# A hybrid decoder block with a PEER mixer: G tables requested half a group earlier, the residual fetched before the end, hidden products spread, 22 gathered rows moved to an earlier loop, and three places instead of four for the first 56 gathered rows

## The chip, the cores and the metric

The kernel runs on one core of a Trainium2 chip. The core has a matrix engine (TensorE, PE in the rows; its weight loads are PEld), a vector engine (VectorE, DVE), a scalar engine (ScalarE, ACT), GpSimd (POOL) and SyncE (SP), each with a queue of its own that it works off in order. Loads and stores between device memory and on-chip memory are issued on SP's and POOL's queues, and a few on ACT's. The metric is the device time of one execution in microseconds (us).

## The reference

The block works on 512 tokens of 1024 features (four tiles of 128 tokens). After the two token mixers comes the PEER channel mixer, which most of the change touches: each token picks 8 x 16 experts of 16384 by a product key, and

```
def block(args):
    xb, ib, gb = args
    hid = jnp.einsum('thkd,td->thk', u[ib], xb)
    a = jax.nn.gelu(hid.astype(jnp.float32), approximate=False) * gb
    return jnp.einsum('thk,thkd->td', a.astype(x.dtype), v[ib])
...
x = x + merged @ w_out[layer]
h2 = rms_norm(x, norm2_g[layer])
x = x + peer_ffn(h2, peer_wq[layer], peer_subkeys[layer], peer_u[layer], peer_v[layer])
```

Here `u` and `v` are tables of 16384 rows of 1024 float32 values, `ib` the indices of the picked experts and `gb` their gates.

## The kernel before

The kernel does PEER in two ways at once. For some products it gathers the picked rows, one row of `u` or `v` per token, 128 tokens at a time (512 KB a gather, an indirect DMA on POOL's queue, `row`), and multiplies on VectorE; for the others it streams all of `u` and `v` through TensorE, and a table G that holds the gates in a dense form picks what counts. Token tiles 0 and 3 have their `u` side by gathered rows, tile 3 its `v` side too; tiles 1 and 2 have both sides dense, tile 0 its `v` side.

Time falls into four parts.

1. The front of token tile 0 alone (norm, projections, HGRN2, attention, gates).
2. The front of tiles 1 to 3 (`Front`, `mixers`, `post`), weights streamed through `slot`. Beside it run the 128 gathered `u` rows of tile 0: after each weight load `background` lets the pump `rows` go on by 2.8 rows, up to 128. A gathered row needs a place on chip, given in turn from `row_places`: three buffers named rq and one named row. VectorE's product (`u_steps`, scalar_tensor_tensor with its sum into `hid`) frees the place. After the front, the three rq places take the PEER queries.
3. The hidden loop (`for b in range(NPRE)`, 72 steps): each step multiplies one block of 128 experts of `u` (`hidden`: tile ub, product ph, result pre). Beside it run the routing of the other tiles, the steps that build G (`scatter_steps`: tiles e, eg, pg, Gx; the table goes to device memory as g_d), and `ROWS_H` = 0.6 gathered `u` rows of tile 3 a step.
4. The down loop (`for b in range(NKEY)`, 128 steps): step b takes the slice b of G, which is loaded eight steps at a time (1.5 MB, tile Gc from g_d) into one of two buffers in turn, multiplies it by pre[b] in place (VectorE), splits it into two parts (ah on ScalarE, al on VectorE), loads a block of `v` (tile vb), splits it too (vh on ScalarE, vl on VectorE), and multiplies on TensorE: 18 matmuls of 512 columns into six accumulators acc. The remaining 56 hidden products (24 matmuls of 256 columns each, with ub split into uh and ul) run in the same loop, one a step in program order, and so do `ROWS_D` = 1.9 gathered rows a step, first the rest of the `u` rows, then the 128 `v` rows (`v_steps`).

After the loop three token tiles are finished in turn: the residual is read back from `out`, both accumulators of the tile are added on VectorE, and the tile is stored.

The order of the instructions on each engine is set when the program is built: a scheduler with a time model of its own takes the instructions in program order, moves one ahead where its model says that its inputs and its buffer are ready, and writes one fixed list for each engine. So a list can differ from the code's order, and at run time each engine waits at its next entry, whatever is ready behind it.

Of the kernel before, what the change touches and what calls it, by code (L numbers as in the profile page):

```python
# [8 lines left out]
F32 = mybir.dt.float32  # L9
# [9 lines left out]
P = 128  # L19
S = 512  # L20
D = 1024
# [6 lines left out]
NKEY = 128  # L28
# [13 lines left out]
VD = (1, 2, 0)  # L42
NU = len(UD) * P
GT = 16
NGT = len(VD) * P // GT
GB = 8
# [2 lines left out]

ROWS_F = 2.8  # L50

NPRE, RING = 72, 56

ROUTE1, ROUTE2, SCAT_H = 12, 30, 2
# [1 line left out]
GS = 4  # L56
ACTW = (4, 12)

ROWS_H, ROWS_D = 0.6, 1.9
UBUFS = 3  # L60
UK, WBUFS, WSBUFS, ATB = 4, 2, 4, 2

# [9 lines left out]
def kernel(ctx: ExitStack, tc: tile.TileContext, x, wst, par, cst, cols, g2, keys, u, v, ut, vr, out):  # L72
# [695 lines left out]
    rctx = ctx.enter_context(ExitStack())  # L768
    rt = rctx.enter_context(tc.tile_pool(name="rt", bufs=1, side="left", **TILE))
    pr = rctx.enter_context(tc.tile_pool(name="pr", bufs=1, space=PSUM, side="left"))  # L770
    row_places = [(rq_pool, "rq")] * 3 + [(gat, "row")]

    def background(load):
        rows(min(ROWS_F, P - rows.done))

    f = Front(tuple(range(1, 4)), True, background)
# [17 lines left out]
    def hidden(b, pool):  # L794
        if RING <= b < NPRE:

            if (b - RING) % 4 == 0:
                pre4[0] = rq_pool.tile([P, 4, NU], F32, name="rq") if b - RING < 12 else rq_pool.tile([P, 4, NU], F32, name="keys_sb", bufs=1)
            dst = pre4[0][:, (b - RING) % 4]
        else:  # L800
            dst = dp.tile([P, NU], F32, name="pre", bufs=RING)
        pre.append(dst)
        ub = us.tile([P, KC, P], F32, name="ub")
        nc.sync.dma_start(out=ub, in_=ut[b].rearrange("p (k i) -> p k i", k=KC))
        pt = pool.tile([P, NU], F32, name="ph")
        if b < NPRE:

            accumulate(pt, [ub[:, k] for k in range(KC)], h32, slice(None), True)
        else:
            ubs = halves(us.tile([P, KC, P], F32R, name="uh", bufs=1), us.tile([P, KC, P], F32R, name="ul", bufs=1), ub)  # L810
            accumulate(pt, [tuple(a[:, k] for a in ubs) for k in range(KC)], (hH, hL), slice(None), True)
        return nc.scalar.activation(dst, pt, AF.Gelu)  # L812

    with tc.tile_pool(name="hw", bufs=1, side="right", **TILE) as hw, \
            tc.tile_pool(name="gb", bufs=1, side="left", **TILE) as gb, \
            tc.tile_pool(name="php", bufs=3, space=PSUM, side="right") as php, \
            tc.tile_pool(name="pg", bufs=3, space=PSUM, side="right") as pg:
        pg_bank = lambda: pg.tile([P, 512], F32, name="pg")
        h32 = hw.tile([P, KC, NU], F32, name="h32")
        nc.vector.tensor_tensor(out=h32, in0=hH.bitcast(F32), in1=hL.bitcast(F32), op=ALU.add)  # L820
        scat.add(scatter_steps(0, pg_bank))
        routing(3, rq3)
        rows.add(u_steps(3))
        for b in range(NPRE):
            if b == ROUTE1:
                routing(1, rq1)
                scat.add(scatter_steps(1, pg_bank))
            if b == ROUTE2:
                routing(2, rq2)
                scat.add(scatter_steps(2, pg_bank))  # L830
            behind[:] = [hidden(b, php)]
            rows(ROWS_H)
            if b % SCAT_H == 0:
                scat(1)
        scat(P)
# [6 lines left out]
    ngu = NU // GT  # L842
    acc = [[pacc.tile([P, 512], F32, name=f"acc{t}{c}") for c in range(2)] for t in range(len(VD))]
    for b in range(NKEY):
        if b % GB == 0:
            Gc = Gcs[0]
            if b:
                Gc = (vs if b // GB % 2 else dp).tile([P, NGT, GB, GT], F32, name="Gc", bufs=1)
                nc.sync.dma_start(out=Gc, in_=g_d[:, :, b:b + GB])
        a = pre[b]  # L850
        gsl = Gc[:, :, b % GB]
        nc.vector.tensor_mul(gsl[:, :ngu], a.rearrange("p (g t) -> p g t", t=GT), gsl[:, :ngu])
        aH, aL = halves(vs.tile([P, NGT, GT], F32R, name="ah"), vs.tile([P, NGT, GT], F32R, name="al"), gsl)
        vb = vs.tile([P, D], F32, name="vb", bufs=3)
        nc.sync.dma_start(out=vb, in_=vr[b])
        vH = vs.tile([P, D], F32R, name="vh")
        behind[:] = [nc.scalar.activation(vH, vb, AF.Copy)]  # L857
        vL = vs.tile([P, D], F32R, name="vl")
        nc.vector.tensor_tensor(out=vL, in0=vb, in1=vH.bitcast(F32), op=ALU.subtract)  # L859
        for t in range(len(VD)):  # L860
            for i, (l, r) in enumerate([(aH, vH), (aH, vL), (aL, vH)]):
                for c in range(2):
                    nc.tensor.matmul(acc[t][c], l.rearrange("p g t -> p (g t)")[:, t * P:(t + 1) * P], r[:, c * 512:(c + 1) * 512],  # L863
                                     start=(b == 0 and i == 0), stop=(b == NKEY - 1 and i == 2))
        if b + NPRE < NKEY:
            hidden(b + NPRE, ph)
        rows(ROWS_D)
    rows(2 * S)
    for t, T in enumerate(VD):
        x1r = gat.tile([P, D], F32, name="row")  # L870
        nc.sync.dma_start(out=x1r, in_=out[T * P:(T + 1) * P])
        for c in range(2):
            cs = slice(c * 512, (c + 1) * 512)
            nc.vector.tensor_add(x1r[:, cs], acc[t][c], x1r[:, cs])
        nc.sync.dma_start(out=out[T * P:(T + 1) * P], in_=x1r)


def layout(inputs):
# [53 lines left out]
```

## Time and profile before

| | us |
|---|---|
| median of 3 runs | 1810.34 (1808.81 to 1812.05) |
| the profiled execution | 1805.38 |
| its span (first to last instruction) | 1803.5 |
| TensorE busy | 1639.0 (91% of the span) |
| VectorE busy | 1346.3 (75%) |
| ScalarE busy | 700.8 (39%) |

"Busy" is an average over parts with different limits. A busy TensorE is not one at its peak, since the ends of matmuls are modelled. In a row of idle time the name behind the arrow is what came last before the engine went on.

### The profile page before, as it was taken

What the parts mean: (1) busy time and instruction counts of PE and PEld (TensorE: products, weight loads), DVE (VectorE), ACT (ScalarE), POOL (GpSimd) and SP (SyncE); (2) the same over time, 40 slices, a digit from 0 to 9 for tenths busy, and PEclk for the clock granted to TensorE, in tenths of its full rate; (3) what the DMA queues carried; (4) which work ended last, traced back from release to release, by engine and by line L of the source; (5) the groups of instructions that cost most, each with busy time, mean ns of one, the idle gap of its engine ahead of it and who ended that gap; (6) DMA issues with size and microseconds to landing.
All of it is one profiled execution on the core that took longest, in us unless ns stands there. A gap on an engine that the chain in (4) does not pass through costs nothing.

```text
span 1803.5 us, 26810 instructions
## 1 busy us (share of the span) xinstructions
PE 1639.0 (91%) x9725; PEld 1450.2 (80%) x9725; DVE 1346.3 (75%) x2805; ACT 700.8 (39%) x1283; POOL 641.5 (36%) x502
## 2 busy tenths in 40 slices
PE   8998979789988799999899889999999999988995
PEld 7887968689877797888789877888888888867774
DVE  3113999989886669998985577787788887777774
ACT  3323434334344544523454553334344333323331
POOL 0000355766550004452442123334444444443330
PEclk9999979999989899999999999999999999989998
DMA  8776468788884336665667688999999998888885
GB/s 287 245 232 221 143 206 312 245 296 306 304 287 170 119 121 240 208 201 193 211 227 252 225 293 308 331 355 333 331 335 342 331 331 315 286 281 300 299 293 183
DMA packets 173380, 473.41 MB, mean 262 GB/s; under 512 B 14784, under 2 KB 62144, under 8 KB 173248
## 3 DMA queue, kind: packets, MB, share of 16 engines
q1 hardware_dynamic: 115840, 268.47, 43.9%
q0 software_dynamic: 55296, 201.35, 31.3%
q10 hardware_dynamic: 2112, 1.88, 0.3%
q8 instruction: 77, 1.26, 0.3%
q14 instruction: 55, 0.45, 0.1%
HBM read 442.80 MB, written 27.79 MB: 261 GB/s over the span
## 4 chain that ended last, share of the span: by engine, by line
PE 47%; DVE 25%; DMA 21%; issue 4%; ACT 2%; POOL 1%; DVEq 0%; POOLq 0%; ACTq 0%; SPq 0%
PE acc L863 18%; PE pp L110 16%; DMA Gc<-g_d 9%; PE ph L110 9%; DMA w<-in_wst_dram 2%; DMA rq<-in_u_dram,idx 2%; DVE e L687 2%; DVE rowx L648 2%; PE pg L701 2%; DMA rowx<-in_u_dram,idx 2%; DVE rq L648 1%; DVE row L648 1%; DVE eg L696 1%; DMA row<-in_u_dram,idx 1%; DVE wl L97 1%
## 5 line engine op out<-in xcount | busy, mean ns | idle before, releaser
L110 PE MATMUL ph<-h,ub 128*128 128x256 f32 x1152 | 265.4, 386 | 0.0
L863 PE MATMUL acc<-vl,ah 128*128 128x512 f32 x768 | 243.5, 398 | 18.0 <-DVE vl L859 18.0
L863 PE MATMUL acc<-vh,al 128*128 128x512 f32 x768 | 244.3, 396 | 0.0
L110 PEld LDWEIGHTS ph<-h,ub 128*128 128x128 f32 x1152 | 219.2, 195 | 29.8 <-issue 0.2
L863 PE MATMUL acc<-vh,ah 128*128 128x512 f32 x768 | 221.1, 396 | 9.8 <-ACT vh L857 9.8
L636 POOL DMA_INDIRECT rowx<-in_u_dram,idx x96 | 122.7, 1278 | 216.1 <-ACT pre L812 56.8
L636 POOL DMA_INDIRECT rowx<-in_v_dram,idx x96 | 130.7, 1362 | 193.2 <-DVE h2g L667 90.2
L863 PEld LDWEIGHTS acc<-vl,ah 128*128 128x128 f32 x768 | 145.2, 192 | 49.3 <-DVE vl L859 20.8
L863 PEld LDWEIGHTS acc<-vh,ah 128*128 128x128 f32 x768 | 143.9, 191 | 38.8 <-ACT vh L857 11.1
L863 PEld LDWEIGHTS acc<-vh,al 128*128 128x128 f32 x768 | 146.5, 192 | 30.5
L96 ACT ACTIVATE ah<-Gc 128x384 fp32r<-128x384 f32 x128 | 67.0, 524 | 264.0 <-PE acc L863 261.3
L859 DVE TENSOR_TENSOR vl<-vb,vh 128x1024 fp32r<-128x1024 f32 x128 | 156.1, 1219 | 11.6 <-ACT vh L857 11.2
L857 ACT ACTIVATE vh<-vb 128x1024 fp32r<-128x1024 f32 x128 | 135.6, 1060 | 45.3 <-DMA vb<-in_vr_dram 44.5
L636 POOL DMA_INDIRECT rq<-in_u_dram,idx x96 | 120.0, 1250 | 93.5 <-DVE rq L648 52.9
L648 DVE SCALAR_TENSOR_TENSOR rowx<-rowx,h2g 128x1024 f32<-128x1024 f32 x96 | 122.4, 1276 | 39.2 <-DMA rowx<-in_u_dram,idx 39.1
L648 DVE SCALAR_TENSOR_TENSOR rq<-rq,h2g 128x1024 f32<-128x1024 f32 x96 | 132.8, 1385 | 19.8 <-DMA rq<-in_u_dram,idx 19.6
L96 ACT ACTIVATE wh<-w 128x512 fp32r<-128x512 f32 x144 | 89.1, 629 | 128.8 <-PE pp L110 71.1
L110 PE MATMUL ph<-hH,ul 128*128 128x256 f32 x448 | 127.6, 285 | 5.1 <-DVE ul L97 5.1
L110 PE MATMUL ph<-hH,uh 128*128 128x256 f32 x448 | 127.8, 285 | 3.8 <-ACT pre L812 3.8
L667 DVE SCALAR_TENSOR_TENSOR h2g<-rowx,hid,h2g 128x1024 f32<-128x1024 f32 x95 | 121.7, 1281 | 8.4 <-DMA rowx<-in_v_dram,idx 8.0
L110 PE MATMUL ph<-hL,uh 128*128 128x256 f32 x448 | 127.7, 285 | 0.0
L701 PE MATMUL pg<-eg,e 128*128 128x128 f32 x768 | 104.5, 290 | 23.5 <-DVE eg L696 17.3
(289 smaller groups left out, 3611.9 us busy)
## 6 DMA issues: line engine op xcount, KB each, us to landing
ub<-in_ut_dram SPq DMA_DIRECT2D x128, 512.0 KB, 4.7
vb<-in_vr_dram SPq DMA_DIRECT2D x128, 512.0 KB, 7.1
w<-in_wst_dram SPq DMA_DIRECT2D x107, 512.0 KB, 5.2
g_d<-Gx SPq DMA_DIRECT2D x24, 960.0 KB, 4.6
Gc<-g_d SPq DMA_DIRECT2D x15, 1536.0 KB, 16.5
wh<-in_wst_dram SPq DMA_DIRECT2D x37, 256.0 KB, 4.9
wl<-in_wst_dram SPq DMA_DIRECT2D x33, 256.0 KB, 5.4
pairB<-in_x_dram SPq DMA_DIRECT2D x5, 512.0 KB
```

What stands on the lines that cost most here:

```text
L96: nc.scalar.activation(hi, x, AF.Copy)
L97: (eng or nc.vector).tensor_tensor(out=lo, in0=x, in1=hi.bitcast(F32), op=ALU.subtract)
L110: nc.tensor.matmul(out, l, r, start=(k == 0 and i == 0), stop=(k == last and i == len(ops) - 1))
L636: d = nc.gpsimd.indirect_dma_start(out=r, out_offset=None, in_=src, in_offset=bass.IndirectOffsetOnAxis(ap=index, axis=0))
L648: nc.vector.scalar_tensor_tensor(r, r, 1.0, h2g[T], op0=ALU.mult, op1=ALU.mult, accum_out=hid[:, g, j:j + 1])
L667: nc.vector.scalar_tensor_tensor(acc, r, hid[:, g, j:j + 1], acc, op0=ALU.mult, op1=ALU.add)
L687: nc.vector.tensor_tensor(out=e1, in0=iota[:, None, :, 0].to_broadcast(by_token), in1=pk[:, ti, 0, tk, None].to_broadcast(by_token), op=AL ...
L696: nc.vector.tensor_tensor(out=eg, in0=e2.rearrange("p k q -> p q k"), in1=pkw[:, ti, tk, None].to_broadcast(by_token), op=ALU.mult)
L701: nc.tensor.matmul(pt[:, q], e1[:, q0 + q], eg[:, q0 + q], start=True, stop=True)
L857: behind[:] = [nc.scalar.activation(vH, vb, AF.Copy)]
L859: nc.vector.tensor_tensor(out=vL, in0=vb, in1=vH.bitcast(F32), op=ALU.subtract)
L863: nc.tensor.matmul(acc[t][c], l.rearrange("p g t -> p (g t)")[:, t * P:(t + 1) * P], r[:, c * 512:(c + 1) * 512], start=(b == 0 and i == 0 ...
```

## The change

Five things change. The load of a group of G is written at the middle of the group before it, not at the group's first step. The 56 hidden products of the down loop are spread so that the last is written at step 120 and not at step 55. From step 40 the hidden loop pumps 1.3 rows a step (`ROWS_L`) and no longer 0.6, which moves 22 rows out of the down loop, where 1.6 a step are pumped and no longer 1.9. The residual of the three last tiles is read back at step 123 into the buffers that gathered rows used, and each half of a tile is stored by itself. And the first 56 gathered rows beside the front of tiles 1 to 3 are given the three rq places in turn; the row place joins after them.

```diff
+RFEW = 56
-ROWS_H, ROWS_D = 0.6, 1.9
+ROWS_H, HLATE, ROWS_L, ROWS_D = 0.6, 40, 1.3, 1.6
+ULAST, XLAST = 120, 123
...
-    row_places = [(rq_pool, "rq")] * 3 + [(gat, "row")]
+    row_places = [(rq_pool, "rq")] * 3
     def background(load):
+        if rows.done >= RFEW and len(row_places) < 4:
+            row_places.append((gat, "row"))
         rows(min(ROWS_F, P - rows.done))
...
-            rows(ROWS_H)
+            rows(ROWS_H if b < HLATE else ROWS_L)
...
     for b in range(NKEY):
-        if b % GB == 0:
-            Gc = Gcs[0]
-            if b:
-                Gc = (vs if b // GB % 2 else dp).tile([P, NGT, GB, GT], F32, name="Gc", bufs=1)
-                nc.sync.dma_start(out=Gc, in_=g_d[:, :, b:b + GB])
+        if b % GB == GB // 2 and b + GB < NKEY:
+            g = b // GB + 1
+            Gcs.append((vs if g % 2 else dp).tile([P, NGT, GB, GT], F32, name="Gc", bufs=1))
+            nc.sync.dma_start(out=Gcs[g], in_=g_d[:, :, g * GB:(g + 1) * GB])
+        Gc = Gcs[b // GB]
...
-        if b + NPRE < NKEY:
-            hidden(b + NPRE, ph)
+        if len(pre) < NKEY and (len(pre) - NPRE) * ULAST <= b * (NKEY - NPRE):
+            hidden(len(pre), ph)
         rows(ROWS_D)
-    rows(2 * S)
+        if b == XLAST:
+            rows(2 * S)
+            x1s = []
+            for T in VD:
+                x1s.append(rx.tile([P, D], F32, name="rowx"))
+                nc.sync.dma_start(out=x1s[-1], in_=out[T * P:(T + 1) * P])
     for t, T in enumerate(VD):
-        x1r = gat.tile([P, D], F32, name="row")
-        nc.sync.dma_start(out=x1r, in_=out[T * P:(T + 1) * P])
         for c in range(2):
             cs = slice(c * 512, (c + 1) * 512)
-            nc.vector.tensor_add(x1r[:, cs], acc[t][c], x1r[:, cs])
-        nc.sync.dma_start(out=out[T * P:(T + 1) * P], in_=x1r)
+            nc.vector.tensor_add(x1s[t][:, cs], acc[t][c], x1s[t][:, cs])
+            nc.sync.dma_start(out=out[T * P:(T + 1) * P, cs], in_=x1s[t][:, cs])
```

Three places in the built lists. The first is VectorE's list around the multiplications of steps 96 to 103 (`Gc<-pre,Gc`). The first row is the last reader of the buffer that their load reuses, the al of step 87; the load on SP waits for it in both programs. Before:

```order
L97 TENSOR_TENSOR al<-Gc,ah 128x384
L859 TENSOR_TENSOR vl<-vb,vh 128x1024
L667 SCALAR_TENSOR_TENSOR h2g<-rowx,hid,h2g 128x1024
L667 SCALAR_TENSOR_TENSOR h2g<-row,hid,h2g 128x1024
L667 SCALAR_TENSOR_TENSOR h2g<-rowx,hid,h2g 128x1024
L97 TENSOR_TENSOR al<-Gc,ah 128x384
L859 TENSOR_TENSOR vl<-vb,vh 128x1024
L852 TENSOR_TENSOR Gc<-pre,Gc 128x16x16 x8
```

The same place in the changed program, from the same reader on:

```order
L102 TENSOR_TENSOR al<-Gc,ah 128x384
L867 TENSOR_TENSOR vl<-vb,vh 128x1024
L102 TENSOR_TENSOR al<-Gc,ah 128x384
L867 TENSOR_TENSOR vl<-vb,vh 128x1024
L860 TENSOR_TENSOR Gc<-pre,Gc 128x16x16 x8
L102 TENSOR_TENSOR ul<-ub,uh 128x1024
L672 SCALAR_TENSOR_TENSOR h2g<-rowx,hid,h2g 128x1024
```

Between the reader and the multiplications stood six instructions and now stand three. The table counts the same for all groups from the third on: what stands between the last reader of the buffer and the first multiplication (r a gathered row's product, V a vl, A an al, U a ul, ? the closing of the u rows), and how many r, V, A, U the list has from this group's first multiplication to the next group's.

| group (first step) | between, before | between, now | r,V,A,U before | r,V,A,U now |
|---|---|---|---|---|
| 16 | UVrAVrrUA | rVrArVAV | 15,9,8,5 | 13,8,8,3 |
| 24 | VrAVrUrAV | VrUrAVrAV | 14,8,8,5 | 13,8,8,4 |
| 32 | VrrAUrVAV | VrArVUrAV | 15,8,8,5 | 13,8,8,4 |
| 40 | VrAVrUrAV | rVrAVrUAV | 14,8,8,5 | 13,8,8,3 |
| 48 | VrAVrUrAV | VrUrAV?rAV | 14,8,8,5 | 12,7,7,4 |
| 56 | VrrAU?VrAV | rVUrAV | 14,8,8,5 | 13,8,8,4 |
| 64 | VrrUrAVAV | rVrAVU | 15,8,8,5 | 14,9,9,3 |
| 72 | rVrUrAVrAV | VrAVrAV | 13,7,7,5 | 12,7,7,4 |
| 80 | rVrUrAV | VrrUAV | 15,8,8,5 | 13,8,8,4 |
| 88 | VrUrArV | VrrAVU | 15,8,8,4 | 12,8,8,3 |
| 96 | VrrrAV | VAV | 13,9,9,0 | 13,7,8,4 |
| 104 | rVrArVAV | rVUA | 12,8,8,0 | 13,9,8,4 |
| 112 | VrArVrAV | rVrUAV | 11,8,8,0 | 13,8,8,3 |
| 120 | VrArVrAV | VrAV | to the end: 14 steps, no U | to the end: 15 steps, 4 U |

The second place is the end of the gathered rows of tile 0 on POOL's list, from the last split of a weight half (wl) to the first copy of the hidden loop. Before:

```order
L97 TENSOR_TENSOR wl<-w,wh 128x512
L636 DMA rq<-in_u_dram,idx 128x1024 x2
L636 DMA row<-in_u_dram,idx 128x1024
L636 DMA rq<-in_u_dram,idx 128x1024 x3
L636 DMA row<-in_u_dram,idx 128x1024
```

And in the changed program, from the last use of the row place on:

```order
L641 DMA row<-in_u_dram,idx 128x1024
L641 DMA rq<-in_u_dram,idx 128x1024 x3
L102 TENSOR_TENSOR wl<-w,wh 128x512
L641 DMA rq<-in_u_dram,idx 128x1024 x28
L710 COPY Gc<-Gx 128x128 x2
```

The scheduler uses the row place for later rows early, from the ninth gather on, and so the row place is spent when 31 rows are left. All in all 110 of the 128 gathers now use the three rq places, where 96 did. The third place is the end of SP's list; first before, after the last vb load but one group:

```order
L855 DMA vb<-in_vr_dram 128x1024 x14
L670 DMA row<-out_dram 128x1024
L672 DMA out_dram<-row 128x1024
L871 DMA row<-out_dram 128x1024
L875 DMA out_dram<-row 128x1024
L871 DMA row<-out_dram 128x1024
L875 DMA out_dram<-row 128x1024
L871 DMA row<-out_dram 128x1024
L875 DMA out_dram<-row 128x1024
```

And now:

```order
L863 DMA vb<-in_vr_dram 128x1024 x4
L883 DMA rowx<-out_dram 128x1024
L863 DMA vb<-in_vr_dram 128x1024 x2
L883 DMA rowx<-out_dram 128x1024 x2
L675 DMA row<-out_dram 128x1024
L863 DMA vb<-in_vr_dram 128x1024 x2
L677 DMA out_dram<-row 128x1024
L863 DMA vb<-in_vr_dram 128x1024 x4
L888 DMA out_dram<-rowx 128x512 x6
```

The three reads of the residual have moved among the last vb loads, and only six half stores stand behind them.

## Rows read from the trace of the kernel before

**Rows 1.** The page's head: span and busy time of each engine.

```profile
span 1803.5 us, 26810 instructions
PE 1639.0 (91%) x9725; PEld 1450.2 (80%) x9725; DVE 1346.3 (75%) x2805; ACT 700.8 (39%) x1283; POOL 641.5 (36%) x502
```

**Rows 2.** Busy time by stretch of the down loop (two stretches). Columns: stretch, its length, busy time and count of PE, PEld, DVE, ACT, POOL, then the granted clock, the DMA engines' share, GB/s.

```profile
1110.00:1480.00 370.00, 364.85 (x2034) 318.28 (x2035) 302.46 (x412) 144.04 (x202) 155.02 (x111) 1.00 0.93 332
1480.00:1660.00 180.00, 162.12 (x795) 136.71 (x794) 135.50 (x155) 58.50 (x81) 75.73 (x52) 0.95 0.84 294
```

**Rows 3.** The list of waits from 1050 us on: engine, line, what ended the wait, then total us, times, longest.

```profile
DVE Gc L852 <- DMA Gc<-g_d: 86.9, 15, 8.9
PE acc L863 <- DVE vl L859: 18.0, 6, 8.2
```

**Rows 4.** Timeline of VectorE and SP around three G loads (those of steps 88, 96 and, first row, 16; the last row is that of step 120). Columns: start, us, engine, line, what, and in brackets the idle time before and what ended it.

```profile
1111.67 0.43 DVE L852 TENSOR_TENSOR Gc<-pre,Gc 128x256 f32<-128x256 f32 x1 [8.62 <-DMA Gc<-g_d]
...
1529.65 0.55 DVE L97 TENSOR_TENSOR al<-Gc,ah 128x384 fp32r<-128x384 f32 x1
1530.23 0.53 SPq L849 DMA_DIRECT2D Gc<-g_d  x1
1537.08 1.22 DVE L859 TENSOR_TENSOR vl<-vb,vh 128x1024 fp32r<-128x1024 f32 x1
1545.94 1.10 DVE L852 TENSOR_TENSOR Gc<-pre,Gc 128x256 f32<-128x256 f32 x3 [7.64 <-DMA Gc<-g_d]
...
1580.69 0.53 SPq L849 DMA_DIRECT2D Gc<-g_d  x1
1596.93 2.77 DVE L852 TENSOR_TENSOR Gc<-pre,Gc 128x256 f32<-128x256 f32 x8 [8.87 <-DMA Gc<-g_d]
1602.55 1.22 PE L863 MATMUL acc<-vl,ah 128*128 128x512 f32 x2 [8.20 <-DVE vl L859]
...
1721.36 1.43 DVE L852 TENSOR_TENSOR Gc<-pre,Gc 128x256 f32<-128x256 f32 x4 [6.63 <-DMA Gc<-g_d]
```

**Rows 5.** Groups of VectorE instructions from 1110 to 1727 us: shapes, count, busy us, mean ns of one, idle before.

```profile
L859 DVE TENSOR_TENSOR vl<-vb,vh 128x1024 fp32r<-128x1024 f32 x106 | 129.2, 1219 | 8.3 <-ACT vh L857 8.0
L667 DVE SCALAR_TENSOR_TENSOR h2g<-rowx,hid,h2g 128x1024 f32<-128x1024 f32 x82 | 105.0, 1281 | 8.4 <-DMA rowx<-in_v_dram,idx 8.0
L97 DVE TENSOR_TENSOR ul<-ub,uh 128x1024 fp32r<-128x1024 f32 x49 | 59.8, 1220 | 10.4 <-ACT uh L96 10.1
L97 DVE TENSOR_TENSOR al<-Gc,ah 128x384 fp32r<-128x384 f32 x106 | 58.6, 553 | 16.4 <-ACT ah L96 9.3 <-PE acc L863 6.8
```

**Rows 6.** DMA issues: what, queue, count, KB each, median us from issue to landing; the last row is from the view of the line that loads Gc, over its 15 loads.

```profile
Gc<-g_d SPq DMA_DIRECT2D x15, 1536.0 KB, 16.5
rq<-in_u_dram,idx POOLq DMA_INDIRECT x96, 6.3
...
  DMA to landing us min/median/max: 15.2/16.5/18.0
```

**Rows 7.** TensorE in the down loop: two successive starts of the six vh-by-ah matmuls of a step without a hidden product (timeline), and one hidden product's 22 last matmuls on the chain that ended last.

```profile
1772.68 1.52 PE L863 MATMUL acc<-vh,ah 128*128 128x512 f32 x6
1776.76 1.52 PE L863 MATMUL acc<-vh,ah 128*128 128x512 f32 x6
...
1120.44 2.59 PE ph L110 x22
```

**Rows 8.** The end of the program on the timeline: the last matmuls, the adds, SP's stores and loads.

```profile
1783.31 1.29 DVE L874 TENSOR_TENSOR row<-acc,row 128x512 f32<-128x512 f32 x2 [4.03 <-PE acc L863]
1784.47 0.61 PE L863 MATMUL acc<-vh,al 128*128 128x512 f32 x2
1784.63 0.34 SPq L875 DMA_DIRECT2D out_dram<-row  x1
1787.26 0.33 SPq L871 DMA_DIRECT2D row<-out_dram  x1
1790.94 1.29 DVE L874 TENSOR_TENSOR row<-acc,row 128x512 f32<-128x512 f32 x2 [6.34 <-DMA row<-out_dram]
1799.73 0.34 SPq L875 DMA_DIRECT2D out_dram<-row  x1
```

**Rows 9.** The gathered rows beside the front of tiles 1 to 3, on the timeline: the gather with which the last 31 begin, a gather, its product, the place's next gather, a product that VectorE waited for, and the last product.

```profile
470.99 0.94 POOL L636 DMA_INDIRECT rq<-in_u_dram,idx  x1 [1.21 <-DVE rq L648]
...
502.28 1.15 POOL L636 DMA_INDIRECT rq<-in_u_dram,idx  x1 [1.60 <-DVE rq L648]
509.74 1.23 DVE L648 SCALAR_TENSOR_TENSOR rq<-rq,h2g 128x1024 f32<-128x1024 f32 x1 [1.04 <-DMA rq<-in_u_dram,idx]
512.09 1.21 POOL L636 DMA_INDIRECT rq<-in_u_dram,idx  x1 [0.30 <-DVE at L417]
...
542.01 1.23 DVE L648 SCALAR_TENSOR_TENSOR rq<-rq,h2g 128x1024 f32<-128x1024 f32 x1 [2.80 <-DMA rq<-in_u_dram,idx]
...
548.10 1.22 DVE L648 SCALAR_TENSOR_TENSOR row<-row,h2g 128x1024 f32<-128x1024 f32 x1
```

**Rows 10.** Busy time by stretch in the front of tiles 1 to 3 (first four rows) and in the hidden loop; columns as in Rows 2.

```profile
190.00:300.00 110.00, 94.86 (x667) 90.29 (x665) 106.68 (x297) 43.94 (x75) 59.26 (x45) 0.91 0.64 219
300.00:400.00 100.00, 80.83 (x535) 73.46 (x535) 92.49 (x179) 35.17 (x79) 68.16 (x52) 0.92 0.81 271
400.00:500.00 100.00, 99.00 (x780) 87.22 (x778) 86.69 (x169) 40.69 (x90) 60.50 (x49) 0.98 0.89 307
500.00:562.00 62.00, 48.57 (x318) 42.09 (x317) 53.76 (x102) 25.25 (x41) 22.67 (x19) 0.83 0.72 244
880.00:920.00 40.00, 36.85 (x200) 32.82 (x200) 39.62 (x130) 20.48 (x40) 16.58 (x14) 0.96 0.56 195
960.00:1024.00 64.00, 64.00 (x379) 58.60 (x378) 33.45 (x62) 34.13 (x75) 13.42 (x14) 1.00 0.71 233
```

## The prediction

> **What bounds the kernel now.** I read the page's head first: TensorE is busy 91% of the span of 1803.5 us, VectorE 75% [rows 1]. That alone would say "TensorE is the bound", so I looked stage by stage. In the down loop TensorE needs 4.08 us for a step's 18 matmuls (two successive starts, 1776.76 − 1772.68) and 24 × 2.59/22 = 2.83 us for a hidden product [rows 7]. Eight steps with five hidden products need 46.8 us; the groups' multiplications followed each other every 50 us around step 96, where almost no hidden product is left (1545.94 to 1596.93 is 51.0) [rows 4]. Something else sets that pace.
>
> The list of waits names it: VectorE stood 86.9 us for the loads of G, at 15 loads of 15 [rows 3]. The timeline shows why [rows 4]. After the last al that reads a G buffer (1529.65), SP issues the load into that buffer (1530.23); it lands 16.5 us later at the median, 15.2 to 18.0 [rows 6]; the eight multiplications of the new group stand only a few instructions behind that al in VectorE's list, so VectorE reaches them early and stands (7.64 us before 1545.94). Everything behind them waits too, the al that releases the next buffer among it. This is a ring: release, load, multiply, a group of vector work, release. Its period is
>
> (VectorE's work from one group's first multiplication to the next group's) − (the part that stands between release and multiplication) + 16.5.
>
> With a gathered product 1.28, vl and ul 1.22, al 0.55 [rows 5] and eight multiplications 2.77 [rows 4], group 80 has 15 r, 8 V, 8 A, 5 U = 42.2; between release and multiplication for group 88 stand 3 r, 2 V, U, A = 8.05; so 42.2 − 8.05 + 16.5 = 50.7. Group 88 to 96: 41.0 − 6.8 + 16.5 = 50.7, where the trace has 51.0. Over the 13 periods from group 16 to 120 the formula, with the counts of the table in the section on the change, gives 607.6; the trace has 1721.36 − 1111.67 = 609.7 [rows 4]. I trust it.
>
> **Loads ahead.** The load is written half a group earlier, but the built lists do not follow: SP still waits for the same al, the buffer's last reader, since there are two buffers in both programs. Cost and gain nil by themselves; what counts is the order on VectorE.
>
> **Down loop, groups 16 to 120.** What stands between release and multiplication shrinks at most groups (group 96: VrrrAV, 6.8, becomes VAV, 3.0; group 104: 8.6 becomes 4.3), and that part was work done during the load. The rows are fewer (13 a group for 14), but ul's stay to the end (3 to 4 a group, where before there were five and then none). Group 96 to 104 now: 13 r, 7 V, 8 A, 4 U and 2.77 = 37.2, less 4.3, plus 16.5 = 49.5 (before 43.3). The same for all, now: 43.9, 45.2, 45.2, 43.9, 45.2, 48.2, 49.5, 45.2, 48.2, 49.5, 49.5, 49.4, 49.5, together 612.3. TensorE's need per period, 8 × 4.08 + 3.5 × 2.83 = 42.5, is below each. Before, the first eight periods were 46.4 to 50.2, and the last three 43.3, 40.2, 38.9: the early gain is given back late. Term: 612.3 − 607.6 = +4.7. The period ahead (group 8 to 16), by the same formula, −1.3.
>
> **Down loop, its end.** From the multiplications of the last group on, TensorE's own work decides. Before, 1721.36 to the last matmul at 1785.1 [rows 4, 8] is 63.7 = 14 steps × 4.08 + 6.6 for a restart. Now 15 steps and four hidden products are left: 15 × 4.08 + 4 × 2.83 + 6.6 = 79.1. Term +15.4. Nothing hides it. That is where the spread of u is paid: not in work, but in hidden products that stand behind the last load and not in front of it. Loop in all: +18.8.
>
> **Tail.** Before, behind the last matmul come three rounds of read, two adds and a store in turn (the second round's adds start at 1790.94, 7.6 after the first's at 1783.31, having waited 6.34 for the read), the last store issued at 1799.73, and 3.8 us to the span's end at 1803.5 [rows 1, 8]. Now the reads are done earlier; six adds of 0.645 (1.29/2) from 1783.3 end at 1787.2; plus 3.8 is 1791.0. Term −12.5. The reads move in among the last vb loads; three of 512 KB against a G load's 1536 KB in 16.5 cost no more than one more such load there (bounds 0 to 16), and no G load is left behind them: I take 0.
>
> **Front of tiles 1 to 3.** In the built list 110 gathers and not 96 use the three rq places, and the last 31 use nothing else. A place goes round in product 1.2, reissue 0.3 to 1.1, landing 6.3 [rows 6, 9], 8.2 to 9.0 with the waits in line; the example takes 512.09 − 502.28 = 9.8. With three places that is 2.74 to 3.0 us a row, and 3.3 by the example. Now the last 31 rows run at (548.10 − 470.99)/31 = 2.49 [rows 9]. So they take 8 to 16 us longer, 24 by the example. VectorE already waits for such a gather (2.80 us at 542.01) [rows 9], and splits of the last weights stand behind the last product in its list, with TensorE behind them: between 500 and 562 TensorE is busy 48.6 of 62 us [rows 10]. Against that, VectorE is 97% busy at 190 to 300 (106.7 of 110) [rows 10] and paced by itself, so three places cost little there, and part of the end's loss is slack. Bounds 0 and 24; I take +9, near the lower price of the cycle.
>
> **Hidden loop.** Twenty-two more products of 1.22 to 1.28 come after step 40. From 960 on VectorE is busy 33.5 of 64 us and TensorE all of it: there they are hidden. But six of them stand between two of the G-building steps near 900, where VectorE is busy 39.6 of 40 [rows 10]: 6 × 1.22 = 7.3 if TensorE has no work ahead, 0 if it has. Were the later cover gone, all 22 would cost 27. I take +5, bounds 0 and 12.
>
> **Sum.** 18.8 − 12.5 + 9 + 5 = +20.3 on the profiled execution of 1805.4, that is 1825.7. The median of the three runs is 5 us above that execution, so I say 1830.
>
> **The rivals.** All but the last two terms hang on the landing time of G: each us of it is some 13 to 14 us, one for each period.
>
> 1. *The G loads land sooner: faster.* Fewer gathered rows run beside them (13 of 512 KB a group for 14 to 15) and fewer ub in the first half. The sign turns where the landing falls by 20.3/13.5 = 1.5 us, at 15.0. At 13.5 the time is 1830 − 40 = 1790. At 12 periods touch TensorE's 42.5, and no more is to be had than some 60. For it: the DMA engines were 93% busy up to 1480 and 84% after [rows 2], and the two late loads that I can read landed in 15.7 and 16.2. Against it: these two were below the median by 0.8 at most, although VectorE stood 7.6 and 8.9 us for them and asked for no new rows meanwhile [rows 4]; and from step 89 on ub loads now run beside G where none did. Chance 0.23.
>
> The Trainium skill (DMA: Bandwidth & Descriptors, section on SWDGE, HWDGE and iDMA) says that an engine goes round in turn among its internal queues, those fed by GpSimd apart from those fed by SP. By that a G load would speed up as soon as GpSimd's gathers run dry; an even half of the 294 GB/s of the late stretch would be an estimated 1.57 MB/147 = 10.7 us, and the loop TensorE's, some 60 us shorter. The trace does not bear this out, with 15.7 and 16.2 us for the late loads; other loads stand on SP's own queue.
>
> 2. *Front and hidden loop cost nothing* (slack takes both): 1830 − 14 = 1816. For: the idle 13 us of TensorE between 500 and 562. Chance 0.08.
>
> 3. *The places cost their full price*, 24, and the late reads of the residual hold a vb load up by some us: 1830 + 15 + 3 = 1848. For: the example cycle of 9.8. Chance 0.14.
>
> **Numbers.** My forecast, 1812 to 1846, has 0.55. 1830 is its middle. To hold 8 in 10, the range goes to half of rival 1's side and to rival 3: 1798 to 1849. What a measurement can tell from no change is 0.2%, 1806.7 to 1814.0. Faster takes nearly all of rival 1 (0.23) and a little more where terms fall together (0.02): 0.25; same 0.10, the margins of rivals 1 and 2 and my lower end; slower the rest, 0.65.
>
> **What would show it.** In the changed profile: VectorE's wait for G grows from 86.9 to about 115 us, at every load; periods of 44 to 49.5 with the late ones longest; landing at 16 to 17; hidden products near the last steps and 79 us from the last group's multiplications to the last matmul; 6 us from the last matmul to the end, not 18; the last product of the gathered rows some 9 us later than 548; a longer stretch around 900. I am wrong if the wait for G shrinks, if the last landing times are below 15, or if VectorE's order leaves TensorE enough work queued to ride through the stalls.

## The result and the profile after

The changed kernel is slower: 1824.9 us median for 1810.2 us before, ratio 1.0103, 95% interval 1.0073 to 1.0134. The forecast was 1830 us, with a range of 1798 to 1849. The size came out nearly as forecast, but two of the terms behind it were far off and cancelled, which was luck; so most of this section and the next is on where the time really went. Every ratio here is worked out over all executions in the faster of the chip's two states, and not from the medians (here 14.7 us apart); two of the six executions of e9_rows_moved were in the slower one, its profile among them.

The head of the changed kernel's page answers to [rows 1]:

```profile
span 1823.2 us, 26818 instructions
PE 1648.7 (90%) x9725; PEld 1454.9 (80%) x9725; DVE 1346.7 (74%) x2805; ACT 702.3 (39%) x1284; POOL 646.6 (35%) x502
```

The engines do the same work; what grew is time in which they stand, and, by 9.7 us, TensorE's busy time for the same 9725 matmuls. To find the place, I took the same instructions from the timeline of both kernels: the first gathered row of tile 0, the first matmul of the hidden loop, the first multiplication of the down loop, the last matmul. Before (the last matmul is in [rows 8], at 1784.47 + 0.61):

```profile
215.33 1.30 POOL L636 DMA_INDIRECT rq<-in_u_dram,idx  x1 [1.19 <-DVE idx L603]
650.38 1.99 PE L110 MATMUL ph<-h,ub 128*128 128x256 f32 x8
1048.82 1.43 DVE L852 TENSOR_TENSOR Gc<-pre,Gc 128x256 f32<-128x256 f32 x4 [3.20 <-POOL Gc L705]
```

After, with the last product of the gathered rows (583.43) and the six adds of the tail (1816.08):

```profile
222.87 1.30 POOL L641 DMA_INDIRECT rq<-in_u_dram,idx  x1 [1.20 <-DVE idx L608]
491.44 1.55 POOL L641 DMA_INDIRECT rq<-in_u_dram,idx  x1 [0.30 <-issue]
583.43 1.22 DVE L653 SCALAR_TENSOR_TENSOR rq<-rq,h2g 128x1024 f32<-128x1024 f32 x1
678.39 1.78 PE L115 MATMUL ph<-h,ub 128*128 128x256 f32 x7
1080.40 1.77 DVE L860 TENSOR_TENSOR Gc<-pre,Gc 128x256 f32<-128x256 f32 x5 [3.54 <-POOL Gc L710]
1816.08 3.68 DVE L887 TENSOR_TENSOR rowx<-acc,rowx 128x512 f32<-128x512 f32 x6 [3.80 <-PE acc L871]
1817.46 0.61 PE L871 MATMUL acc<-vh,al 128*128 128x512 f32 x2
```

| stretch | before | after | difference | forecast |
|---|---|---|---|---|
| to the first gathered row | 215.3 | 222.9 | +7.5 | 0 |
| on to the first hidden matmul | 435.1 | 455.5 | +20.5 | +9 |
| hidden loop | 398.4 | 402.0 | +3.6 | +5 |
| down loop, first multiplication to last matmul | 736.3 | 737.7 | +1.4 | +18.8 |
| last matmul to the end | 18.4 | 5.1 | −13.3 | −12.5 |

The instruction lists of all engines are alike up to the first gathered row, so the first difference is not the change's: in the profiles of the experiments below this row stands anywhere between 214.9 and 220.2 us. The rest, +12, is one execution against one other; the ratio over all executions, 1.0103, is +19 us. Two large rows show the miss: the front (first gathered row to first hidden matmul) cost over twice the forecast, and the down loop, in this pair of profiles, nearly nothing. The ratios of many executions put the two loops together at some +12 us (e1_four against e3_tail below, 0.68 points, give or take 0.4), where these profiles have +5 and the forecast 23.8.

The list of waits of the changed kernel, from 1050 us on, answers to [rows 3] (what waited, what ended it, total, times, longest):

```profile
POOL rowx L641 <- ACT vh L865: 148.8, 49, 8.8
...
DVE Gc L860 <- DMA Gc<-g_d: 78.5, 13, 12.3
...
POOL row L641 <- ACT vh L865: 38.2, 15, 4.4
...
DVE h2g L672 <- DMA rowx<-in_v_dram,idx: 28.2, 21, 3.4
...
DVE h2g L672 <- DMA row<-in_v_dram,idx: 23.4, 8, 7.1
...
PE acc L871 <- DVE vl L867: 20.5, 8, 7.5
```

and of the kernel before, the rows that answer to those of POOL and of the v rows:

```profile
POOL rowx L636 <- ACT vh L857: 28.6, 8, 12.2
POOL row L636 <- ACT vh L857: 6.1, 3, 4.7
DVE h2g L667 <- DMA rowx<-in_v_dram,idx: 8.0, 11, 1.4
DVE h2g L667 <- DMA row<-in_v_dram,idx: 0.7, 1, 0.7
```

The wait for G did not grow to 115 us but fell a little. A wait that was no part of the prediction grew instead: VectorE waits 51.6 us for gathered v rows, 8.7 before, and POOL waits 187 us for vh before it issues gathered rows, 34.7 before.

How the G loads behave, on the timeline, answering to [rows 4]: the multiplications of group 16; issue and multiplications of a load in the middle; last reader's al, issue and multiplications of step 96's load; the multiplications of group 120:

```profile
1136.08 2.77 DVE L860 TENSOR_TENSOR Gc<-pre,Gc 128x256 f32<-128x256 f32 x8 [4.35 <-DMA Gc<-g_d]
...
1292.33 0.53 SPq L856 DMA_DIRECT2D Gc<-g_d  x1
1304.99 1.43 DVE L860 TENSOR_TENSOR Gc<-pre,Gc 128x256 f32<-128x256 f32 x4
...
1567.85 0.59 DVE L102 TENSOR_TENSOR al<-Gc,ah 128x384 fp32r<-128x384 f32 x1
1568.46 0.53 SPq L856 DMA_DIRECT2D Gc<-g_d  x1
1583.51 2.77 DVE L860 TENSOR_TENSOR Gc<-pre,Gc 128x256 f32<-128x256 f32 x8 [12.34 <-DMA Gc<-g_d]
...
1740.57 1.09 DVE L860 TENSOR_TENSOR Gc<-pre,Gc 128x256 f32<-128x256 f32 x3 [9.26 <-DMA Gc<-g_d]
```

Release, load, wait is there as described: with only VAV (3.0 us) between, VectorE stood 12.34 us at step 96. But a load could be in after less than 12.7 us in the middle, where VectorE did not stand at all (1304.99). From group 16 to 120 it is 1740.57 − 1136.08 = 604.5 us, where the formula said 612.3. From there to the last matmul (1818.1) it is 77.5, forecast 79.1.

### The profile page after: what moved, and what is told of

The parts are those of the page before. It is cut to its first block, busy times and chain, and to the rows that moved or that the text cites. A ratio compares the mean times of both kernels' runs of the same rounds, so it can differ in the third digit from the quotient of the medians.

```text
span 1823.2 us, 26818 instructions
## 1 busy us (share of the span) xinstructions
PE 1648.7 (90%) x9725; PEld 1454.9 (80%) x9725; DVE 1346.7 (74%) x2805; ACT 702.3 (39%) x1284; POOL 646.6 (35%) x502
## 4 chain that ended last, share of the span: by engine, by line
PE 36%; DVE 27%; DMA 22%; issue 9%; POOL 4%; ACT 1%; DVEq 0%; ACTq 0%; POOLq 0%; SPq 0%
PE pp L115 16%; PE acc L871 14%; DMA Gc<-g_d 9%; PE ph L115 4%; DVE rowx L653 3%; DMA rq<-in_u_dram,idx 3%; DMA rowx<-in_v_dram,idx 3%; DMA w<-in_wst_dram 2%; DVE e L692 2%; DMA row<-in_u_dram,idx 2%; DVE h2g L672 2%; DVE rq L653 2%; DMA rowx<-in_u_dram,idx 1%; POOL rq L641 1%; DVE eg L701 1%
## 5 line engine op out<-in xcount | busy, mean ns | idle before, releaser
L871 PE MATMUL acc<-vl,ah 128*128 128x512 f32 x768 | 241.5, 396 | 20.7 <-DVE vl L867 20.5
L871 PE MATMUL acc<-vh,al 128*128 128x512 f32 x768 | 240.2, 394 | 0.0
L641 POOL DMA_INDIRECT rowx<-in_v_dram,idx x96 | 151.0, 1573 | 232.0 <-ACT vh L865 118.3
L641 POOL DMA_INDIRECT rq<-in_u_dram,idx x110 | 130.5, 1187 | 130.1 <-DVE rq L653 83.0
L653 DVE SCALAR_TENSOR_TENSOR rq<-rq,h2g 128x1024 f32<-128x1024 f32 x110 | 145.4, 1327 | 33.9 <-DMA rq<-in_u_dram,idx 32.7
```

Source lines behind the costliest of these rows:

```text
L641: d = nc.gpsimd.indirect_dma_start(out=r, out_offset=None, in_=src, in_offset=bass.IndirectOffsetOnAxis(ap=index, axis=0))
L653: nc.vector.scalar_tensor_tensor(r, r, 1.0, h2g[T], op0=ALU.mult, op1=ALU.mult, accum_out=hid[:, g, j:j + 1])
```

## The experiments

Each is a change of one of the two kernels; ratios are to the kernel before, run on the same chip. "Points" are hundredths of that ratio, some 18 us each.

**Four places (label e1_four).** On the changed kernel:

```diff
-RFEW = 56
+RFEW = 0
```

> The changed kernel with the row place in turn from the first gathered row on (four places throughout, as before the change); all else as changed. Theory A (the three places cost the front its time): the gathered rows of tile 0 end near 555 us and not near 585, the hidden loop begins at 650 to 660 us and not at 678, the down loop and the end stay, so the time is 1825 - 20 to 28 = 1797 to 1805 us, below the kernel before. Theory B (most of the 28 us in the front is drift between executions or VectorE being full): hidden loop begins at 668 or later, time 1814 to 1825 us.

Measured 1807.2 us, ratio 1.0001 (0.9973 to 1.0028). Of the change's +1.03%, 1.02 points are the place. First gathered row and first hidden matmul:

```profile
218.28 1.30 POOL L641 DMA_INDIRECT rq<-in_u_dram,idx  x1 [1.21 <-DVE idx L608]
656.36 1.99 PE L115 MATMUL ph<-h,ub 128*128 128x256 f32 x8
```

438.1 us between them, for 455.5 in the changed kernel and 435.1 before. That is theory A for the front. Its time, 1797 to 1805 us and below the kernel before, was missed: without the three places the change gains nothing, although its tail alone gains 12 us (e3_tail below).

**Three places alone (e2_three).** On the kernel before:

```diff
-    row_places = [(rq_pool, "rq")] * 3 + [(gat, "row")]
+    row_places = [(rq_pool, "rq")] * 3
     def background(load):
+        if rows.done >= 56 and len(row_places) < 4:
+            row_places.append((gat, "row"))
```

> The kernel before with the three places for the first 56 rows alone; nothing else changed. Theory A: the gathered rows end 20 to 28 us later, and so does all behind them; the down loop's own formula gives 603 for 608 us; time 1810 + 15 to 28 = 1825 to 1838 us. Theory B (the place is not what holds the front): within 8 us of 1810.

Measured 1827.2 us, ratio 1.0107 (1.0068 to 1.0145): +19 us, the same from the other side.

```profile
215.09 1.30 POOL L636 DMA_INDIRECT rq<-in_u_dram,idx  x1 [1.19 <-DVE idx L603]
671.83 1.35 PE L110 MATMUL ph<-h,ub 128*128 128x256 f32 x5
```

456.7 us between them. The periods from group 16 to 120 add up to 607.3 us, where the formula said 603.

**The tail alone (e3_tail).** On the kernel before, the `b == XLAST` block and the stores by halves, as in the diff above. 

> The kernel before with the residual read at step 123 and stores by halves alone. Theory A: the stretch from the last matmul to the span's end falls from 18.4 us to 5 to 6, nothing else moves, so 1797 us. Theory B (the three reads hold the last loads of v up): the last group to the last matmul takes over 68 us for 63.7, time 1802 us or more.

Measured 1795.0 us, ratio 0.9933 (0.9905 to 0.9961): −12 us, theory A; the last group to the last matmul took 63.0 us.

**Hidden products early again (e4_uearly).** On the changed kernel:

```diff
-ULAST, XLAST = 120, 123
+ULAST, XLAST = 55, 123
```

> The changed kernel with the hidden products of the down loop one a step again (the last written at step 55). Theory A (the ring with 16.5 us of landing): from the last group's multiplications to the last matmul 64 us for 77.5, but the periods from group 16 to 120 add up to 626 by the formula, where 612 were worked out for the changed kernel (604.5 seen): down loop about equal, time 1822 to 1830 us. Theory B (landing falls to 13 us, as several loads of the changed kernel showed): the periods are TensorE's, 46 to 47 with five hidden products and 38 to 44 late, sum below 595, time 1800 to 1812 us.

Measured 1842.7 us, ratio 1.0184 (1.0136 to 1.0233): 0.8 points, 15 us, above the changed kernel. Both theories missed: the last stretch is 61.7 us, near the 64 of theory A, but the periods add up to 637.2, 11 more than its formula said and 32.7 more than the changed kernel's 604.5. So the spread of u is a gain in this kernel, though it lengthens the end by 16 us.

**Rows as before (e5_rows).** On the changed kernel:

```diff
-ROWS_H, HLATE, ROWS_L, ROWS_D = 0.6, 40, 1.3, 1.6
+ROWS_H, HLATE, ROWS_L, ROWS_D = 0.6, 72, 0.6, 1.9
```

> The changed kernel with the gathered rows of the hidden and down loops as before (0.6 and 1.9 a step); three places in the front, u spread and tail as changed. Theory A (the ring): the hidden loop is 4 us shorter, the periods from group 16 to 120 add up to 584 by the formula with 16.5 us of landing, where the changed kernel's list gave 612 and the trace 604.5, the last stretch stays near 79: time 1825 - 20 to 30 = 1795 to 1805 us. Theory B (in this half of the loop TensorE is busy 98% and the matrix work sets the pace): the sum stays at 598 or more, time 1815 to 1825 us.

Measured 1794.5 us, ratio 0.9942 (0.9923 to 0.9961): 1.61 points, 29 us, below the changed kernel, with the three places still in. The multiplications of groups 16 and 120, and then two rows of the list of waits from 1050 us on:

```profile
1125.56 1.77 DVE L860 TENSOR_TENSOR Gc<-pre,Gc 128x256 f32<-128x256 f32 x5 [5.72 <-DMA Gc<-g_d]
1708.12 1.10 DVE L860 TENSOR_TENSOR Gc<-pre,Gc 128x256 f32<-128x256 f32 x3 [5.71 <-DMA Gc<-g_d]
```

```profile
POOL rowx L641 <- ACT vh L865: 24.5, 6, 11.9
...
DVE h2g L672 <- DMA rowx<-in_v_dram,idx: 14.7, 16, 2.7
```

1708.12 − 1125.56 = 582.6, where the formula said 584. Theory A, and the dearest part of the down loop's change is found: the 22 rows that were moved out of it.

**Rows moved alone (e9_rows_moved).** The reverse, on the kernel before:

```diff
-ROWS_H, ROWS_D = 0.6, 1.9
+ROWS_H, HLATE, ROWS_L, ROWS_D = 0.6, 40, 1.3, 1.6
...
-            rows(ROWS_H)
+            rows(ROWS_H if b < HLATE else ROWS_L)
```

> The kernel before with the 22 gathered rows moved alone (0.6 a step to step 40 of the hidden loop, 1.3 after, 1.6 in the down loop). Theory A (the ring: with fewer rows the list puts less work between release and multiplication): the formula with 16.5 us of landing gives 631 us for the periods from group 16 to 120, where the kernel before has 608; hidden loop 3 to 5 us longer; with landing a little shorter, as in the runs so far, time 1805 + 15 to 25 = 1820 to 1830 us, slower. Theory B (less work in a loop is less time): 1795 to 1805 us.

Measured 1853.0 us, ratio 1.0235 (1.0174 to 1.0297): +42 us, theory A in sign, and 17 us beyond its upper end. Twenty-two products of 1.28 us less in a loop made it longer. In the profile the periods from group 16 to 120 add up to 653.7 us, 23 more than the formula's 631, and VectorE and POOL wait for more than G:

```profile
DVE Gc L852 <- DMA Gc<-g_d: 106.5, 15, 11.6
POOL rowx L636 <- ACT vh L857: 215.9, 60, 9.4
DVE h2g L667 <- DMA rowx<-in_v_dram,idx: 34.8, 19, 4.7
```

**Multiplications of G later (e6_late).** On the kernel before, one edge in VectorE's own order (`als` holds the al of each step; that split is written out in place for it, unchanged):

```diff
...
-        nc.vector.tensor_mul(gsl[:, :ngu], a.rearrange("p (g t) -> p g t", t=GT), gsl[:, :ngu])
+        with tc.issue_after(als[b - 3].ins) if b >= GB else ExitStack():
+            nc.vector.tensor_mul(gsl[:, :ngu], a.rearrange("p (g t) -> p g t", t=GT), gsl[:, :ngu])
```

> The kernel before, where the multiplication of a step's G slice stands behind the al three steps earlier in VectorE's list, so that a G load has six steps to land and not some two; all work stays. Theory A (the ring holds the down loop): VectorE's wait for G falls from 87 us to below 5, and the time by what TensorE stood idle in the down loop, some 20 to 30 us in its late third and up to 10 before: 1770 to 1785 us. Theory B (the whole of the wait was lost time): 1730 to 1750 us. Theory C (the loads of v and the gathered rows set the pace, at 330 GB/s): the wait moves to vb and the rows, time 1800 to 1812 us.

Measured 1792.6 us, ratio 0.9923 (0.9902 to 0.9944). The wait for G is gone, as A said; the longest waits of VectorE from 1050 us on are now for splits on ScalarE:

```profile
DVE ul L97 <- ACT uh L96: 42.8, 23, 4.4
DVE al L857 <- ACT ah L856: 27.8, 34, 2.1
DVE vl L863 <- ACT vh L861: 26.5, 13, 6.7
```

But 87 us of removed wait bought 14 us, between A and C. B is refuted outright. TensorE's idle time in the down loop fell from 35.2 to 19.4 us, no further; VectorE now waits for these others. With five hidden products a group TensorE needs 46.8 us [rows 7], and the periods of the kernel before were 44 to 51 there: over two thirds of the loop the ring was little longer than the matrix work.

**With the new tail (e7_late_tail).** 

> The same as the run before this one and the residual read at step 123 with stores by halves, on the kernel before. If the two parts add up: 12 to 13 us below the run before this one. If the early reads collide with the last loads of v now that the loop runs faster: less than 8 us below it.

Measured 1776.8 us, ratio 0.9835 (0.9809 to 0.9861): 16 us below the run before, within the two intervals of the 12 to 13 expected. The parts add up. Against the tail alone (e3), the late multiplications are worth 18 us here (0.98 points).

**The changed kernel with four places and late multiplications (e8_after_late).** 

> The changed kernel with four places throughout and the multiplications of G three steps ahead of their use. Theory A (u spread and rows moved were right in themselves, and only the ring with late multiplications spoiled them): below the run of the kernel before with late multiplications and the new tail, by 5 us or more. Theory B (hidden products behind the last load lengthen the end whatever the order): above that run by 5 us or more.

Measured 1765.4 us, ratio 0.9785 (0.9752 to 0.9818): 9 us below the run before, as theory A said. That does not show that the moved rows were right in themselves: e11 below, which differs in the rows alone, is 12 us better. The v rows are still waited for:

```profile
POOL rowx L641 <- ACT vh L869: 170.1, 54, 8.8
DVE h2g L672 <- DMA rowx<-in_v_dram,idx: 40.3, 21, 5.0
DVE h2g L672 <- DMA row<-in_v_dram,idx: 14.1, 9, 3.3
```

**The good parts alone (e10_u_tail).** The changed kernel with the edits of e1 and e5 together: four places, rows as before; u spread, loads written ahead and tail stay.

> The changed kernel with four places throughout and the gathered rows of the later loops as before; u spread, loads written ahead and the tail stay. If the parts add up as measured alone: front 20 us better than in the run with three places and rows as before, so 1794 - 20 = 1772 to 1778 us; the periods sum to 581 by the formula. If front and down loop hang together (a loop that starts earlier waits more): 1780 us or more.

Measured 1779.7 us, ratio 0.9849 (0.9808 to 0.9890). That lies between the two expectations, 1.7 us above the first and 0.3 below the second, and does not tell them apart; against e5 four places are worth 0.93 points here, 17 us, for 19 in e1 and e2. The periods add up to 578.2 us, where the formula said 581. Against the tail alone (0.9933) the u spread, with the loads written ahead, is worth −0.84 points, 15 us: the same as from e4. The loads written ahead were not tried alone, and they may not be free of effect: e4 lies 0.86 points, 15 us, below what e9 with places and tail added would give, about as much as the intervals leave open.

**And late multiplications (e11_u_tail_late).** 

> The run before this one with the multiplications of G behind the al three steps earlier. Theory A (in this order the ring already runs at TensorE's 44 us a group, so late multiplications give little more): 0 to 8 us below it. Theory B (the remaining wait for G is all lost): 20 us or more below it.

Measured 1756.5 us, ratio 0.9717 (0.9677 to 0.9758): 24 us below the run before, give or take 10 by the two intervals (the down loops of the two profiles differ by 17.8). Theory B; I had expected A. In e10 the wait for G was still 47.5 us:

```profile
DVE Gc L860 <- DMA Gc<-g_d: 47.5, 13, 5.7
```

In the stretch of the groups 16 to 120 the columns are stretch, length, then busy time and count of PE, PEld, DVE, ACT, POOL, the clock, the DMA share and GB/s; first the kernel before, then e10, then this one:

```profile
1111.00:1721.00 610.00, 583.47 (x3064) 500.77 (x3064) 480.75 (x614) 221.06 (x306) 251.19 (x180) 0.98 0.90 318
```

```profile
1109.00:1687.00 578.00, 565.67 (x3001) 487.52 (x3002) 466.45 (x602) 221.80 (x305) 258.28 (x171) 0.99 0.92 329
```

```profile
1121.00:1684.00 563.00, 563.00 (x3022) 487.20 (x3021) 470.75 (x601) 221.32 (x306) 236.48 (x173) 1.00 0.96 339
```

Here TensorE is busy through and through. In e10 it stood 12 us of this stretch, less than in the kernel before (26), so it was the fuller of the two; what differs is that e6 left 17 us of standing in this stretch, and here none is left. The waits of VectorE for v rows are 5.4 us in all, in place of e8's 54:

```profile
DVE al L865 <- ACT ah L864: 62.1, 62, 2.9
POOL rowx L641 <- ACT vh L869: 30.6, 16, 8.8
DVE h2g L672 <- DMA row<-in_v_dram,idx: 4.7, 3, 2.3
DVE h2g L672 <- DMA rowx<-in_v_dram,idx: 0.7, 1, 0.7
```

**Four steps for a load in place of six (e12_late_more).** `als[b - 5]` for `als[b - 3]`. 

> The same with the multiplications behind the al five steps earlier, which leaves a load of G four steps (some 22 us) and not six. If 16 us is what a load needs: the same as the run before this one within 0.4%, with a wait for G below 10 us. If the loads take longer once VectorE does not stand still: the wait for G comes back, 20 us or more, and the time rises by 5 us or more.

Measured 1754.8 us, ratio 0.9706 (0.9666 to 0.9747): the same as e11, and no wait for a load of G in VectorE's list. The 20 to 26 us from issue to use that the loads then have are enough.

## Why the prediction was right, and where it was not

**The sign and the size** were right, the way to them only half: the front was put 10 us too low, the two loops about as much too high, and that these cancelled was luck. By the ratios, each part beside those named ahead of it: tail −12 us (e3), u spread with the loads −15 (e10 against e3), places +17 (e5 against e10), rows moved +29 (the changed kernel against e5). Together that is the measured +19, and must be, since each step starts where the last ended. The prediction's terms were places +9, tail −12.5, hidden loop +5, down loop +18.8. The parts are not independent: places are +17 to +19 wherever they were tried (e1, e2, e10), but the moved rows cost 42 us on the kernel before (e9), 29 in the changed one, and 12 with late multiplications (e8 against e11).

**The tail** held: −12.5 said, −12 and −13.3 seen, and the reads moved ahead cost nothing that could be seen.

**The front** had the right mechanism and half the size. The step that failed is the choice of a price "near the lower price of the cycle", with nothing for the early stretch. From the gather with which the last 31 rows begin to the start of the last product it is 583.43 − 491.44 = 92.0 us, 2.97 a row and not 2.49, which is +15, close to the upper price of 3.0 a row. The early stretch, called cheap since VectorE was 97% busy there, cost 13 us more: from the first gathered row to the 31st from the end it is 268.6 us for 255.7. That is no drift: the four profiles with three places have 268 to 272 there, the ten with four 255 to 261. Some 7 of these 28 us (15 and 13) were then slack. How the 13 come about is only in part seen: VectorE's idle time in that stretch grew from 19.3 to 28.9 us and POOL's wait for a free rq place from 40.3 to 50.0, but VectorE's waits for gathered rows themselves grew by some 3. That a late gather holds up the splits of weights behind its product in VectorE's list is likely and not shown. A high busy share, at any rate, was no evidence that a lost place is free.

**The hidden loop**: +5 said, +3.6 seen, and +1 to +6 in the other kernels with the moved rows (e1, e8, e4, e9).

**The ring** in the down loop is real: late multiplications make the wait for G vanish and the time shorter (e6, e11, e12). Where 1.9 rows a step are pumped, its formula met lists that it had not seen, to 1.4 us in e5 (584 and 582.6), 3 in e10 and 4 in e2. The step that failed is what I made of it for the changed kernel, where it said 612.3 for 604.5 and a wait for G of about 115 us for 78.5. Two of the prediction's own signs of being wrong came: the wait for G shrank, and of the last four loads two were in use after 13.3 and 14.2 us. It failed in three ways.

First, "with 16.5 us of landing". That figure rests on four landings (18.0, 17.3, 15.2, 15.7): the trace holds no more of the 15 loads. The time from issue to first multiplication, which each load has, has the same median before, 16.5 over the groups 16 to 120, but 14.5 in the changed kernel. The other kernels in which VectorE waits for G part by the rows alone: 16.3 to 16.7 where 1.9 a step are pumped (e2, e3, e5, e10), 13.5 to 14.6 where 1.6 are (e1, e4, e9). That is the mechanism of rival 1, and it took back part of the loss. By the rule of the Trainium skill cited in the prediction (DMA: Bandwidth & Descriptors, section on SWDGE, HWDGE and iDMA) an even half would have been an estimated 10.7 us; from group 16 on the shortest here was 11.6, and in e1, e4 and e9 six loads were in use after 8.9 to 10.8, so the traces went further towards it than the prediction allowed. That the gathers' standstill (POOL waiting for vh) is what freed the engines is likely and was not tested by itself.

Second, the formula knows one wait only, and its total for the changed kernel came near because two errors met. With each kernel's own times from issue to multiplication in place of 16.5, it gives 604.6 for 609.7 us before and 586.4 for 582.6 in e5, but 582.5 for 604.5 in the changed kernel and 587.8 for 637.2 in e4. What is missing there goes with another wait: VectorE waited for gathered rows, 55 us in the changed kernel and 69 in e4, for 23 before. From group 88 to 112 the changed kernel's periods were 52.5, 51.2 and 55.9, where the formula said 49.5, 49.5 and 49.4. The likely cause stands in the code that I read and did not use: a gather gets an edge to the vh of the step at which it was written (`behind`, in `row`), and may not be issued before it. The timelines bear this out. With 1.9 rows a step, rows are written ahead of the place that comes free, and a gather went out a median of 21 us after its vh in the kernel before, 47 to 50 in e5, e10 and e11. With 1.6, it went out a median of 1.6 to 1.9 us after its vh (changed, e1, e4, e8, e9), over two fifths of them within 1.5 us. POOL's waits for vh (34.7 and then 187 us) say the same. e8 and e11, where nobody waits for G and which differ in the rows alone, put 12 us on the moved rows, some 3 of them in the hidden loop. The edge itself was not taken away.

Third, the blame. "That is where the spread of u is paid" is wrong as an account of the whole. The longer end is there (77.5, and 61.7 with u early), but the periods before it are 32.7 us shorter with u spread. The matrix work of the down loop is the same in both; with u early (e4) TensorE stood 49.6 us of the loop, spread 38.5, and its busy time was 707 and 699 us. Why it stands more with u early is open: VectorE waits 13 us more for G there and 14 more for gathered rows. I worked the formula for the whole change only. Worked for each edit alone, from its built lists, it gives 584 for the change without the moved rows and 631 for the moved rows alone on the kernel before, and would have pointed at the rows.

**Rival 2** (front and hidden loop free) fell with e1 and e2. **Rival 3** was nearer than my +9, but neither half of it came: the places cost 17 to 19 us and not 24, and the late reads held nothing up (e3).

## What to carry over

When several edits meet in one order, work the formula for each edit alone before naming a culprit; a total that agrees proves none of its terms. A wait on a vector engine's list is worth only what it takes off the bounding engine's standing, whatever its own length: 87 us of wait were worth 14 to 18 us (e6, e7), where TensorE still stood 17 us of the stretch below, and 47 us were worth 24, give or take 10 (e11), where it stood no more. The stretch of groups 16 to 120, by the profiles:

| | wait for G (whole loop) | length of the stretch | TensorE stood | granted clock |
|---|---|---|---|---|
| e4_uearly | 91.6 | 637.2 | 44.3 | 0.97 |
| changed | 78.5 | 604.5 | 32.9 | 0.97 |
| before | 86.9 | 609.7 | 26.2 | 0.98 |
| e6_late | none | 589.7 | 16.7 | 0.98 |
| e10_u_tail | 47.5 | 578.2 | 12.5 | 0.99 |
| e11_u_tail_late | none | 563.5 | 0.0 | 1.00 |

The last column is a second price of standing. In these traces the clock is granted at one of two levels, 2.4 GHz (1.00) or 1.2, and the figure is the mean of the stretch: the longer TensorE stood, the lower it is, so that TensorE is also busy longer with its matmuls (573 us in e6 for 3026 of them, 563 in e11 for 3024).

And work that is taken out of a loop can slow it down, if it was what filled a latency or what kept a queue ahead: here four places, rows as before, u spread, the new tail and multiplications placed three to five steps ahead give 1755 us, 3% less than the kernel before and 3.9% less than the changed one.

## What the runs showed of the hardware

The same 1.5 MB load took 9.5 to 18.2 us from issue to first multiplication in these two kernels; a mean taken from one kernel missed the next one's by 2 us, some 26 us over 13 loads. And executions of one program differ by about 1%: with equal lists, the first gathered row of tile 0 stood between 214.9 and 222.9 us, so terms under 8 us in one profile need the median of many runs behind them.
